# Sum of ReLU rows: the last 128 rows one to a partition, their sums turned by a transposition and stored in four packets

## The chip, the cores and the metric

One core of a Trainium2 chip. The metric is the device time of one execution in microseconds (us); the kernel before takes 160.97 us, the median of three runs (160.88 to 161.13). ACT is the scalar engine, DVE the vector engine, POOL is GpSimd, SP is the engine that issues all transfers here.

## The reference

```python
# x: float32, 32 x 512 x 1024
relu_x = np.maximum(x, 0)
return np.sum(relu_x, axis=-1).astype(np.float32)     # 32 x 512
```

So 16,384 rows of 1,024 numbers are clamped at zero and each is summed: 67.11 MB are read and 64 KB are written.

## The kernel before

The input is seen as 16,384 rows. The first 2,048 rows are cut so that each of the 128 partitions has 16 rows that lie one behind another in memory (`xf`, line 83). The other 14,336 are cut in the same way into 112 rows for each partition (`xv`, line 84). The sums of a partition stand in a row of the SBUF tensor `res` (128 x 128), in the same order, and so each store writes one piece of memory for each partition.

The loop over `TWO` (lines 183 to 203) works through seven blocks of 16 rows for each partition, 8 MB each, in three buffers in turn. ACT clamps a piece in place (`clamp`, line 144), and DVE sums its rows (`total`, line 152). Of the last two blocks, some rows are done in a single pass: ACT clamps and sums a row in one instruction (`act_row`, line 159), and so does DVE (`dve_row`, line 167). Both write the sum with a second short instruction that reads the engine's accumulator. Then come two smaller loads of 8 and 4 rows (`TAIL`, lines 208 to 218), whose rows alternate between ACT and DVE.

The last four rows of each partition are four loads (lines 220 to 245), all issued on SP's one queue, in this order. Sizes are bytes for each partition:

- 9,208: two whole rows and the first 254 numbers of the third. ACT and DVE do one row each, POOL clamps the 254 numbers (line 234).
- 3,492: the last 873 numbers of the fourth row. ACT sums 321 and DVE 552 of them (`act_part` line 121, `dve_part` line 126).
- 2,072: the next 518 numbers of the third row, 214 on ACT, 304 on DVE.
- 1,612: the last 403 numbers, which end the third row (252 of them) and begin the fourth (151), into a tensor `last` that has free columns at both ends. The partial sums above were written into those columns.

When this last load and all five partial results are there (one semaphore, `all_there`, line 253), DVE's line 254 adds the clamped `last` half to the 254 numbers from POOL and gives the sum of row three, while ACT's line 121 gives the sum of row four. There is no instruction after that: both sums land in two neighbouring columns of `res`.

There are three stores (`store`, line 115), all issued by SP behind all the loads: the first 16 columns (64 bytes for each partition), the next 110 columns (440 bytes), and the last two columns (8 bytes, 128 packets, line 264). SP holds the last of these until DVE and ACT have written. After it SP clears the semaphores, waits until the three stores have landed (line 51), and the kernel is over. `wait_ge` is a wait that is an instruction by itself; `wait_op` hangs a wait on an instruction. The first load is issued ahead of the kernel's opening (line 268).

Of the kernel before, what the change touches and what calls it, by code (L numbers as in the profile page):

```python
# [4 lines left out]
F32 = mybir.dt.float32  # L5
RELU = mybir.ActivationFunctionType.Relu
MAX, ADD = mybir.AluOpType.max, mybir.AluOpType.add
P = 128

ROWS = 16  # L10
# [10 lines left out]

HEAD, MIDDLE = 254, 518
LAST_DVE, LAST_ACT = 252, 151
MIDDLE_ACT, END_ACT = 214, 321

EARLY = 1

# [1 line left out]
def kernel(tc: tile.TileContext, x: bass.AP, out: bass.AP):  # L31
    nc = tc.nc
    sems = Semaphores(tc)

    tc.close()
    tc.compile()
    nc.cur_bb = nc.bb_map[tc.start_bb_name]
    body = nc.cur_bb.bb.instructions
    ends = list(body)
    body.clear()  # L40
    n_stores = relu_sum(nc, sems, x, out)
    body.extend(ends)


    nc.cur_bb = nc.bb_map[tc.start_bb_name + "_end"]
    nc.cur_bb.bb.instructions.clear()
    nums = sorted(s.num for s in (*sems.loads, sems.act, sems.dve))
    cleared = range(nums[0], nums[-1] + 1)
    assert len(cleared) == len(nums)
    nc.sync.sem_clear(cleared)  # L50
    nc.sync.wait_ge(sems.stored, 16 * n_stores).then_inc(sems.stored, -16 * n_stores)
    open_without_barrier(tc, EARLY)


class Semaphores:
    def __init__(self, tc: tile.TileContext):
        n = len(TWO) + len(TAIL) + 4
        self.loads = [tc.alloc_semaphore(f"load{i}") for i in range(n)]
        self.act = tc.alloc_semaphore("act")
        self.dve = tc.alloc_semaphore("dve")  # L60
        self.end = self.loads[-1]
        self.stored = tc.alloc_semaphore("stored")


def relu_sum(nc, sems: Semaphores, x: bass.AP, out: bass.AP):
    x_flat = x.flatten_outer_dims()
    N, D = x_flat.shape
    NT = N // P
    NB = len(TWO)
    assert N == P * NT == P * ROWS * (NB + 1)  # L70
    assert sum(TAIL) == ROWS - 4
    assert HEAD + MIDDLE + LAST_DVE == D and HEAD == 2 + LAST_DVE

    bufs = [nc.alloc_sbuf_tensor(f"io{i}", [P, ROWS, D], F32) for i in range(NBUF)]
    res = nc.alloc_sbuf_tensor("res", [P, NT], F32)


    n_last = LAST_DVE + LAST_ACT
    last = nc.alloc_sbuf_tensor("last", [P, 2 + n_last + 2], F32)


    N1 = P * ROWS
    xf = x_flat[:N1].rearrange("(p m) d -> p m d", p=P)
    xv = x_flat[N1:].rearrange("(p m) d -> p m d", p=P)
    o_flat = out.rearrange("b s -> (b s)")
    of = o_flat[:N1].rearrange("(p m) -> p m", p=P)
    ov = o_flat[N1:].rearrange("(p m) -> p m", p=P)

    def rows(m, n):
        if m < ROWS:  # L90
            return xf[:, m : m + n, :]
        return xv[:, m - ROWS : m - ROWS + n, :]

    def sums(m, n):
        if m < ROWS:
            return of[:, m : m + n], res[:, m : m + n]
        return ov[:, m - ROWS : m - ROWS + n], res[:, m : m + n]
# [3 lines left out]
    def load(dst, src, after=None):  # L101
        nonlocal n_load
        dma = nc.sync.dma_start(out=dst, in_=src)  # L103
        if after:
            dma.wait_op(sems.dve, after[1], "sem-ge")
        dma.then_inc(sems.loads[n_load], 16)
        n_load += 1
        return sems.loads[n_load - 1]

    def store(m, n, act, sem, count):  # L110
        nonlocal n_store
        dst, src = sums(m, n)
        if act:
            nc.sync.wait_ge(sems.act, act)
        nc.sync.dma_start(out=dst, in_=src).wait_op(sem, count, "sem-ge").then_inc(
            sems.stored, 16
        )
        n_store += 1

    def act_part(ap, accum_out, after):  # L120
        nc.scalar.activation(out=ap, in_=ap, func=RELU, accum_out=accum_out).wait_op(  # L121
            *after, "sem-ge"
        ).then_inc(sems.end, 1)

    def dve_part(ap, accum_out, after):
        i = nc.vector.tensor_scalar(  # L126
            out=ap,
            in0=ap,
            scalar1=0.0,
            scalar2=None,  # L130
            op0=MAX,
            op1=ADD,
            accum_out=accum_out,
        )
        if after is not None:
            i.wait_op(*after, "sem-ge")
        i.then_inc(sems.end, 1)

    def clamp(ap, loaded):
        nonlocal n_act  # L140
# [16 lines left out]
    def act_row(ap, accum_out, loaded):  # L157
        nonlocal n_act
        i = nc.scalar.activation(out=ap, in_=ap, func=RELU, accum_out=accum_out)  # L159
        if loaded is not None:  # L160
            i.wait_op(loaded, 16, "sem-ge")
        i.then_inc(sems.act, 1)
        n_act += 1

    def dve_row(ap, accum_out, loaded):
        nonlocal n_dve
        i = nc.vector.tensor_scalar(  # L167
            out=ap,
            in0=ap,
            scalar1=0.0,  # L170
            scalar2=None,
            op0=MAX,
            op1=ADD,
            accum_out=accum_out,
        )
        if loaded is not None:
            i.wait_op(loaded, 16, "sem-ge")
        i.then_inc(sems.dve, 1)
        n_dve += 1

    freed = []
    m = 0
    for j in range(NB):
        buf = bufs[j % NBUF]
        loaded = load(buf[:, :, :], rows(m, ROWS), j >= NBUF and freed[j - NBUF])
        c = 0
# [20 lines left out]
    c = 0  # L207
    for n in TAIL:
        loaded = load(
            buf[:, c : c + n, :], rows(m, n), None if c else freed[NB - NBUF]  # L210
        )
# [6 lines left out]
            m += 1  # L218

    flat = buf[:, :, :].rearrange("p c d -> p (c d)")  # L220
    src = rows(m, 4).rearrange("p c d -> p (c d)")
    at = c * D
    head = 2 * D + HEAD
    middle = head + MIDDLE
    end = middle + n_last


    loaded = load(flat[:, at : at + head], src[:, :head])
    act_row(buf[:, c, :], res[:, m : m + 1], loaded)
    sums_act = n_act  # L230
    dve_row(buf[:, c + 1, :], res[:, m + 1 : m + 2], loaded)
    sums_dve = n_dve
    clamped = flat[:, at + 2 * D : at + head]
    nc.gpsimd.tensor_scalar(  # L234
        out=clamped, in0=clamped, scalar1=0.0, scalar2=None, op0=MAX
    ).wait_op(loaded, 16, "sem-ge").then_inc(sems.end, 1)
    for lo, hi, n, first, second in (
        (end, 4 * D, END_ACT, 2 + n_last, 3 + n_last),
        (head, middle, MIDDLE_ACT, 0, 1),
    ):  # L240
        loaded = load(flat[:, at + lo : at + hi], src[:, lo:hi])
        act_part(flat[:, at + lo : at + lo + n], last[:, first : first + 1], (loaded, 16))
        dve_part(flat[:, at + lo + n : at + hi], last[:, second : second + 1], (loaded, 16))
    loaded = load(last[:, 2 : 2 + n_last], src[:, middle:end])
    assert loaded is sems.end

    store(0, ROWS, freed[0][0], sems.dve, freed[0][1])
    store(ROWS, NT - ROWS - 2, sums_act, sems.dve, sums_dve)  # L250


    all_there = (sems.end, 16 + 5)
    nc.vector.scalar_tensor_tensor(  # L254
        out=clamped,
        in0=last[:, : 2 + LAST_DVE],
        scalar=0.0,
        in1=clamped,
        op0=MAX,
        op1=ADD,  # L260
        accum_out=res[:, NT - 2 : NT - 1],
    ).wait_op(*all_there, "sem-ge").then_inc(sems.end, 1)
    act_part(last[:, 2 + LAST_DVE :], res[:, NT - 1 : NT], all_there)
    store(NT - 2, 2, 0, sems.end, 16 + 5 + 2)
    return n_store


def open_without_barrier(tc: tile.TileContext, n_loads: int):

    SP = mybir.EngineType.SP
    blocks = tc.nc.main_func.blocks
    opening = blocks[0].instructions
    body = next(b for b in blocks if b.name == tc.start_bb_name).instructions
    for i in list(opening):
        if isinstance(i, (mybir.InstDrain, mybir.InstEventSemaphore)):
            opening.remove(i)
    loads = [i for i in body if i.engine == SP][:n_loads]
    for i in loads:  # L280
        assert isinstance(i, mybir.InstDMACopy)
        body.remove(i)
    at = next(n for n, i in enumerate(opening) if i.engine == SP)
    opening[at:at] = loads
# [30 lines left out]
```

## Time and profile before

| what | value |
|---|---|
| median of three runs | 160.97 us (160.88 to 161.13) |
| span of the profiled execution, first to last instruction | 159.695 us (the page rounds to 159.7) |
| what lies around the span, median less span | 1.27 us |
| DMA engines busy | 98.0% of the span, 421 GB/s |
| DVE, ACT, POOL busy | 118.8, 103.6, 1.0 us |
| last load landed, by the trace's semaphore records | 157.749 us |
| last store issued on SP, and landed | 158.262 us, 159.661 us |

Only the span is given of the profiled execution; its own time outside the profiler isn't, so the 1.27 us is a difference between the median and the span. A row of a timeline is the start, the length, the engine, the line and the shape of an instruction, all in us from the span's start. SPq is SP's issue of a transfer; the transfer itself goes on after it. The trace also holds each packet that a DMA engine moved, with its start and size, and the moment at which each engine's semaphore increment arrived.

### The profile page before, as it was taken

The page shows a single profiled execution, that of the slowest core. Times are in us where ns is not written, and L with a number is a line of the kernel's source. Part 1 is how long each engine was busy: PE and PEld are TensorE (multiplying, and loading weights), DVE is VectorE, ACT ScalarE, POOL GpSimd, SP SyncE. Part 2 cuts the span into 40 slices and gives each one's busy share as a digit, 9 for nine tenths or more (in the row PEclk, how much of TensorE's full clock was granted, in tenths as well). Part 3 has the DMA queues.
Part 4 walks back from the last instruction along what each step waited for, and adds up shares of the span by engine and source line. Part 5 has one row for each costly group of instructions (what it writes and reads, how often), then busy time and mean ns, then how long its engine had stood idle before and what let it go on. Part 6 is the DMA issues. An engine that isn't in the chain of part 4 may idle for free.

```text
span 159.7 us, 125 instructions
## 1 busy us (share of the span) xinstructions
DVE 118.8 (74%) x44; ACT 103.6 (65%) x53; POOL 1.0 (1%) x5
## 2 busy tenths in 40 slices
DVE  0000000006999799999999999999999799999986
ACT  0000049993699808996099951999329993496995
POOL 0000000000000000000000000000000000000001
DMA  7996996996997997979969969969969969898993
GB/s 263 525 525 263 525 509 279 525 509 279 525 476 312 525 443 345 525 328 460 525 279 509 525 263 525 525 263 525 509 279 525 492 295 525 353 435 386 407 409 128
DMA packets 2304, 67.18 MB, mean 421 GB/s; under 512 B 640, under 2 KB 768, under 8 KB 1024
## 3 DMA queue, kind: packets, MB, share of 16 engines
q1 hardware_dynamic: 2304, 67.18, 98.0%
HBM read 67.11 MB, written 0.07 MB: 421 GB/s over the span
## 4 chain that ended last, share of the span: by engine, by line
DVE 45%; DMA 45%; ACT 9%; SPq 1%; issue 0%
DMA io<-in_x_dram 45%; DVE res L152 43%; ACT io L144 9%; DVE io L167 1%; SPq L103 1%; DVE io L126 1%; DVE io L254 0%
## 5 line engine op out<-in xcount | busy, mean ns | idle before, releaser
L152 DVE TENSOR_REDUCE res<-io 128x8 f32<-128x8192 f32 (+2 forms) x10 | 101.1, 10175 | 38.9 <-ACT io L144 38.9
L144 ACT ACTIVATE io<-io 128x8192 f32<-128x8192 f32 (+2 forms) x10 | 81.8, 8218 | 25.9 <-DMA io<-in_x_dram 25.9
L159 ACT ACTIVATE io<-io 128x1024 f32<-128x1024 f32 x18 | 18.8, 1043 | 6.6 <-DMA io<-in_x_dram 6.6
L167 DVE TENSOR_SCALAR_CACHE_REDUCE io<-io 128x1024 f32<-128x1024 f32 x14 | 16.2, 1214 | 0.5 <-DMA io<-in_x_dram 0.4
L142 ACT ACT_TABLE_LOAD x1 | 1.3, 1283 | 22.0 <-DMA io<-in_x_dram 22.0
L159 ACT ACTIVATION_READ_ACCUMULATOR io<-io 128x1 f32 x18 | 3.4, 187 | 0.0
L234 POOL TENSOR_SCALAR io<-io 128x254 f32<-128x254 f32 x1 | 0.8, 840 | 155.1 <-DMA io<-in_x_dram 155.1
L167 DVE DVE_READ_ACCUMULATOR io<-io 128x1 f32 x14 | 1.1, 82 | 0.0
L126 DVE TENSOR_SCALAR_CACHE_REDUCE io<-io 128x552 f32<-128x552 f32 (+1 forms) x2 | 1.1, 596 | 0.0
L121 ACT ACTIVATE io<-io 128x321 f32<-128x321 f32 (+1 forms) x2 | 0.9, 426 | 0.1
L254 DVE SCALAR_TENSOR_TENSOR io<-last,io 128x254 f32<-128x254 f32 x1 | 0.4, 425 | 0.0
L121 ACT ACTIVATION_READ_ACCUMULATOR io<-io 128x1 f32 x2 | 0.4, 187 | 0.0
L121 ACT ACTIVATE last<-last 128x153 f32<-128x153 f32 x1 | 0.3, 332 | 0.0
L121 ACT ACTIVATION_READ_ACCUMULATOR last<-last 128x1 f32 x1 | 0.2, 187 | 0.0
L126 DVE DVE_READ_ACCUMULATOR io<-io 128x1 f32 x2 | 0.2, 84 | 0.0
L299 POOL MEMSET const-bfloat16-1.0<- 128x1 bf16 x1 | 0.1, 101 | 0.0
L299 POOL MEMSET const-uint8-127<- 128x1 uint8 x1 | 0.1, 101 | 0.0
L299 POOL MEMSET const-float32-0.0<- 128x1 f32 x1 | 0.1, 99 | 0.2 <-issue 0.2
L299 POOL MEMSET const-float32-1.0<- 128x1 f32 x1 | 0.1, 98 | 0.0
L254 DVE DVE_READ_ACCUMULATOR io<-last,io 128x1 f32 x1 | 0.1, 83 | 0.0
## 6 DMA issues: line engine op xcount, KB each, us to landing
io<-in_x_dram SPq DMA_DIRECT2D x1, 4096.0 KB, 23.8
io<-in_x_dram SPq DMA_DIRECT2D x1, 2048.0 KB, 28.3
io<-in_x_dram SPq DMA_DIRECT2D x1, 1151.0 KB, 30.6
io<-in_x_dram SPq DMA_DIRECT2D x1, 436.5 KB, 31.2
io<-in_x_dram SPq DMA_DIRECT2D x1, 259.0 KB, 31.4
last<-in_x_dram SPq DMA_DIRECT2D x1, 201.5 KB, 31.4
io<-in_x_dram SPq DMA_DIRECT2D x7, 29.1
out_dram<-res SPq DMA_DIRECT2D x1, 55.0 KB, 1.6
```

What stands on the lines that cost most here:

```text
L103: dma = nc.sync.dma_start(out=dst, in_=src)
L121: nc.scalar.activation(out=ap, in_=ap, func=RELU, accum_out=accum_out).wait_op(*after, "sem-ge").then_inc(sems.end, 1)
L126: i = nc.vector.tensor_scalar(out=ap, in0=ap, scalar1=0.0, scalar2=None, op0=MAX, op1=ADD, accum_out=accum_out,)
L142: nc.scalar.preload_act_table(RELU).wait_op(loaded, 16, "sem-ge")
L144: i = nc.scalar.activation(out=ap, in_=ap, func=RELU)
L152: nc.vector.tensor_reduce(out=res[:, m : m + n], in_=ap, axis=mybir.AxisListType.X, op=ADD).wait_op(sems.act, n_act, "sem-ge").then_inc(se ...
L159: i = nc.scalar.activation(out=ap, in_=ap, func=RELU, accum_out=accum_out)
L167: i = nc.vector.tensor_scalar(out=ap, in0=ap, scalar1=0.0, scalar2=None, op0=MAX, op1=ADD, accum_out=accum_out,)
L234: nc.gpsimd.tensor_scalar(out=clamped, in0=clamped, scalar1=0.0, scalar2=None, op0=MAX).wait_op(loaded, 16, "sem-ge").then_inc(sems.end, 1)
L254: nc.vector.scalar_tensor_tensor(out=clamped, in0=last[:, : 2 + LAST_DVE], scalar=0.0, in1=clamped, op0=MAX, op1=ADD, accum_out=res[:, NT ...
L299: nc = _bacc.Bacc("TRN2", target_bir_lowering=False, num_devices=1)
```

## The change

The partition cut of the 14,336 rows becomes one of 14,208: each partition has 111 rows of them, and the last 128 rows of the input (`xl`) are given one to each partition. Of the last four rows of a partition, the third is now finished before the last, from the 254 numbers that POOL clamped (DVE, `scalar_tensor_tensor`), its 516 last numbers (ACT) and an addition of both on POOL. The fourth, from `xl`, comes in two loads of 573 and 451 numbers. The loads of the end are therefore 9,208, 3,080, 2,292 and 1,804 bytes for each partition, again four.

The sum of that last row is made of two halves, as before a piece on ACT (180 numbers) and a piece on DVE (271 numbers and the two partial sums of the first 573). Then DVE adds the halves into column 0 of `column`, a 128 x 32 tensor that POOL zeroed at the start, and transposes it in blocks of 32 x 32 into `across`. Row 0, 32, 64 and 96 of `across` hold 32 sums each, which are neighbours in the output. The last store writes these four rows, 128 bytes each, instead of 8 bytes from each of 128 partitions. The second store now carries 111 columns (444 bytes) and waits for POOL's addition.

```diff
@@ -21,9 +21,11 @@
-HEAD, MIDDLE = 254, 518
-LAST_DVE, LAST_ACT = 252, 151
-MIDDLE_ACT, END_ACT = 214, 321
+HEAD = 254
+HEAD_ACT = 516
+FIRST, FIRST_ACT = 573, 240
+LAST_ACT = 180
+BLOCK = 32
 EARLY = 1
@@ -44,7 +46,7 @@
     nc.cur_bb = nc.bb_map[tc.start_bb_name + "_end"]
     nc.cur_bb.bb.instructions.clear()
-    nums = sorted(s.num for s in (*sems.loads, sems.act, sems.dve))
+    nums = sorted(s.num for s in (*sems.loads, sems.act, sems.dve, sems.pool, sems.fin))
     cleared = range(nums[0], nums[-1] + 1)
     assert len(cleared) == len(nums)
     nc.sync.sem_clear(cleared)
@@ -58,6 +60,8 @@
         self.loads = [tc.alloc_semaphore(f"load{i}") for i in range(n)]
         self.act = tc.alloc_semaphore("act")
         self.dve = tc.alloc_semaphore("dve")
+        self.pool = tc.alloc_semaphore("pool")
+        self.fin = tc.alloc_semaphore("fin")
         self.end = self.loads[-1]
         self.stored = tc.alloc_semaphore("stored")
@@ -69,22 +73,29 @@
     NB = len(TWO)
     assert N == P * NT == P * ROWS * (NB + 1)
     assert sum(TAIL) == ROWS - 4
-    assert HEAD + MIDDLE + LAST_DVE == D and HEAD == 2 + LAST_DVE
+    assert HEAD + HEAD + HEAD_ACT == D
     bufs = [nc.alloc_sbuf_tensor(f"io{i}", [P, ROWS, D], F32) for i in range(NBUF)]
     res = nc.alloc_sbuf_tensor("res", [P, NT], F32)
-    n_last = LAST_DVE + LAST_ACT
-    last = nc.alloc_sbuf_tensor("last", [P, 2 + n_last + 2], F32)
+    n_last = D - FIRST
+    split = nc.alloc_sbuf_tensor("split", [P, FIRST], F32)
+    last = nc.alloc_sbuf_tensor("last", [P, 2 + n_last], F32)
+    halves = nc.alloc_sbuf_tensor("halves", [P, 4], F32)
+    column = nc.alloc_sbuf_tensor("column", [P, BLOCK], F32)
+    across = nc.alloc_sbuf_tensor("across", [P, BLOCK], F32)
     N1 = P * ROWS
     xf = x_flat[:N1].rearrange("(p m) d -> p m d", p=P)
-    xv = x_flat[N1:].rearrange("(p m) d -> p m d", p=P)
+    N2 = N - P
+    xv = x_flat[N1:N2].rearrange("(p m) d -> p m d", p=P)
+    xl = x_flat[N2:]
     o_flat = out.rearrange("b s -> (b s)")
     of = o_flat[:N1].rearrange("(p m) -> p m", p=P)
-    ov = o_flat[N1:].rearrange("(p m) -> p m", p=P)
+    ov = o_flat[N1:N2].rearrange("(p m) -> p m", p=P)
+    ol = o_flat[N2:].rearrange("(b i) -> b i", i=BLOCK)
     def rows(m, n):
         if m < ROWS:
@@ -116,25 +127,6 @@
             sems.stored, 16
         )
         n_store += 1
-
-    def act_part(ap, accum_out, after):
-        nc.scalar.activation(out=ap, in_=ap, func=RELU, accum_out=accum_out).wait_op(
-            *after, "sem-ge"
-        ).then_inc(sems.end, 1)
-
-    def dve_part(ap, accum_out, after):
-        i = nc.vector.tensor_scalar(
-            out=ap,
-            in0=ap,
-            scalar1=0.0,
-            scalar2=None,
-            op0=MAX,
-            op1=ADD,
-            accum_out=accum_out,
-        )
-        if after is not None:
-            i.wait_op(*after, "sem-ge")
-        i.then_inc(sems.end, 1)
     def clamp(ap, loaded):
         nonlocal n_act
@@ -178,6 +170,7 @@
         i.then_inc(sems.dve, 1)
         n_dve += 1
+    nc.gpsimd.memset(column[:, :], 0.0).then_inc(sems.pool, 1)
     freed = []
     m = 0
     for j in range(NB):
@@ -218,50 +211,77 @@
             m += 1
     flat = buf[:, :, :].rearrange("p c d -> p (c d)")
-    src = rows(m, 4).rearrange("p c d -> p (c d)")
+    src = rows(m, 3).rearrange("p c d -> p (c d)")
     at = c * D
     head = 2 * D + HEAD
-    middle = head + MIDDLE
-    end = middle + n_last
+    end = 3 * D
     loaded = load(flat[:, at : at + head], src[:, :head])
     act_row(buf[:, c, :], res[:, m : m + 1], loaded)
-    sums_act = n_act
     dve_row(buf[:, c + 1, :], res[:, m + 1 : m + 2], loaded)
-    sums_dve = n_dve
     clamped = flat[:, at + 2 * D : at + head]
     nc.gpsimd.tensor_scalar(
         out=clamped, in0=clamped, scalar1=0.0, scalar2=None, op0=MAX
-    ).wait_op(loaded, 16, "sem-ge").then_inc(sems.end, 1)
-    for lo, hi, n, first, second in (
-        (end, 4 * D, END_ACT, 2 + n_last, 3 + n_last),
-        (head, middle, MIDDLE_ACT, 0, 1),
-    ):
-        loaded = load(flat[:, at + lo : at + hi], src[:, lo:hi])
-        act_part(flat[:, at + lo : at + lo + n], last[:, first : first + 1], (loaded, 16))
-        dve_part(flat[:, at + lo + n : at + hi], last[:, second : second + 1], (loaded, 16))
-    loaded = load(last[:, 2 : 2 + n_last], src[:, middle:end])
-    assert loaded is sems.end
-
-
-
-    store(0, ROWS, freed[0][0], sems.dve, freed[0][1])
-    store(ROWS, NT - ROWS - 2, sums_act, sems.dve, sums_dve)
-
-
-    all_there = (sems.end, 16 + 5)
+    ).wait_op(loaded, 16, "sem-ge").then_inc(sems.pool, 1)
+
+
+    loaded = load(flat[:, at + head : at + end], src[:, head:end])
+    act_row(flat[:, at + head + HEAD : at + end], halves[:, 1:2], loaded)
+    raw = flat[:, at + head : at + head + HEAD]
+    nc.vector.wait_ge(sems.pool, 2)
     nc.vector.scalar_tensor_tensor(
         out=clamped,
-        in0=last[:, : 2 + LAST_DVE],
+        in0=raw,
         scalar=0.0,
         in1=clamped,
         op0=MAX,
         op1=ADD,
-        accum_out=res[:, NT - 2 : NT - 1],
-    ).wait_op(*all_there, "sem-ge").then_inc(sems.end, 1)
-    act_part(last[:, 2 + LAST_DVE :], res[:, NT - 1 : NT], all_there)
-    store(NT - 2, 2, 0, sems.end, 16 + 5 + 2)
+        accum_out=halves[:, 0:1],
+    ).wait_op(loaded, 16, "sem-ge").then_inc(sems.dve, 1)
+    n_dve += 1
+    nc.gpsimd.wait_ge(sems.act, n_act)
+    nc.gpsimd.tensor_tensor(
+        out=res[:, m + 2 : m + 3], in0=halves[:, 0:1], in1=halves[:, 1:2], op=ADD
+    ).wait_op(sems.dve, n_dve, "sem-ge").then_inc(sems.pool, 1)
+
+
+    loaded = load(split[:, :], xl[:, :FIRST])
+    act_row(split[:, :FIRST_ACT], last[:, 0:1], loaded)
+    dve_row(split[:, FIRST_ACT:], last[:, 1:2], loaded)
+    loaded = load(last[:, 2:], xl[:, FIRST:])
+    assert loaded is sems.end
+
+
+    store(0, ROWS, freed[0][0], sems.dve, freed[0][1])
+    store(ROWS, NT - ROWS - 1, 0, sems.pool, 3)
+
+
+    cut = 2 + n_last - LAST_ACT
+    nc.scalar.activation(
+        out=last[:, cut:], in_=last[:, cut:], func=RELU, accum_out=halves[:, 2:3]
+    ).wait_op(loaded, 16, "sem-ge").then_inc(sems.fin, 1)
+    nc.vector.wait_ge(sems.act, n_act)
+    nc.vector.wait_ge(sems.dve, n_dve)
+    nc.vector.tensor_scalar(
+        out=last[:, :cut],
+        in0=last[:, :cut],
+        scalar1=0.0,
+        scalar2=None,
+        op0=MAX,
+        op1=ADD,
+        accum_out=halves[:, 3:4],
+    ).wait_op(loaded, 16, "sem-ge").then_inc(sems.fin, 1)
+    nc.vector.tensor_tensor(
+        out=column[:, 0:1], in0=halves[:, 2:3], in1=halves[:, 3:4], op=ADD
+    ).wait_op(sems.fin, 2, "sem-ge").then_inc(sems.fin, 1)
+    nc.vector.transpose(out=across[:, :], in_=column[:, :]).wait_op(
+        sems.fin, 3, "sem-ge"
+    ).then_inc(sems.fin, 1)
+    nc.sync.dma_start(out=ol, in_=across[::BLOCK, :]).wait_op(
+        sems.fin, 4, "sem-ge"
+    ).then_inc(sems.stored, 16)
+    n_store += 1
     return n_store
```

## The prediction

> **What bounds the kernel now.** I read the page's first three parts, then the chain that ended last, then the timeline of the last 4 us, then SP's waits. The first three say that the transfers are the bound:
>
> ```profile
> span 159.7 us, 125 instructions
> DVE 118.8 (74%) x44; ACT 103.6 (65%) x53; POOL 1.0 (1%) x5
> q1 hardware_dynamic: 2304, 67.18, 98.0%
> ```
>
> The one queue that everything goes through keeps its engines busy for 98.0% of the span, while DVE has 26% of it free. The trace's packet records show the pace: a 65,536-byte packet takes 2.418 us, 27.1 bytes per ns on each of 16 engines. So no change to compute matters until the last load has landed; the change doesn't take a byte away. What can move the end is what stands behind that landing. The timeline shows it:
>
> ```profile
> 156.73 1.86 SPq L115 DMA_DIRECT2D out_dram<-res  x2
> ...
> 157.29 0.38 ACT L121 ACTIVATE io<-io 128x214 f32<-128x214 f32 x1
> 157.29 0.47 DVE L126 TENSOR_SCALAR_CACHE_REDUCE io<-io 128x304 f32<-128x304 f32 x1
> 157.58 0.19 ACT L121 ACTIVATION_READ_ACCUMULATOR io<-io 128x1 f32 x1
> 157.69 0.08 DVE L126 DVE_READ_ACCUMULATOR io<-io 128x1 f32 x1
> 157.80 0.33 ACT L121 ACTIVATE last<-last 128x153 f32<-128x153 f32 x1
> 157.80 0.42 DVE L254 SCALAR_TENSOR_TENSOR io<-last,io 128x254 f32<-128x254 f32 x1
> 158.04 0.19 ACT L121 ACTIVATION_READ_ACCUMULATOR last<-last 128x1 f32 x1
> 158.15 0.08 DVE L254 DVE_READ_ACCUMULATOR io<-last,io 128x1 f32 x1
> ```
>
> The last load's final semaphore increment arrives at 157.749 by the trace. Both engines start 0.05 us later, at 157.80, and end at 158.23 and 158.235. SP's issue of the last store starts at 158.262 (the second half of the first row above), 0.027 us behind DVE. What follows is the store alone:
>
> ```profile
> SPq L115 <- DVE io L254: 1.2, 1, 1.2
> ...
> L115 SPq DMA_DIRECT2D out_dram<-res x3: 332/344/404, 126.9 to 158.3; - x3
> ...
> out_dram<-res SPq DMA_DIRECT2D x1, 1.0 KB, 1.4
> ```
>
> SP waited 1.2 us for DVE, issued in 0.332 us, and the 1.0 KB landed 1.4 us after the issue began: 158.262 to 159.661. SP's end follows 0.034 us later, at 159.695. So behind the landing lie 0.054 + 0.432 of compute, 0.027 of handing over, 1.399 of store and 0.034 of end: 1.946 us. My sum is on these.
>
> The packet records split the store's 1.399: 0.825 from the start of the issue to the first packet (159.087), 0.189 to the start of the last of 128 packets (159.276; each engine has eight, of 9 ns), some 0.006 to the last semaphore packet (159.282), then 0.379 to the last increment.
>
> **The loads.** The four last loads carried 9,208 + 3,492 + 2,072 + 1,612 bytes for each partition and will carry 9,208 + 3,080 + 2,292 + 1,804, the same 16,384 in the same four packets. Packets of the old sizes took 347, 139, 86 and 68 ns, which is 8.5 ns + bytes/27.1; the three new ones come to 122, 93 and 75, 290 against 293. Eight to an engine, that is 0.02 us less: I put the last landing at 157.75 as before. The two between come at about 156.45 and 157.19 (156.586 - 8 x 0.017, and 157.266 - 8 x 0.010). The partitions' distance in memory falls from 112 rows to 111, and the last 128 rows lie one row apart. The first block, 16 rows apart, runs at the same 2.418 us a packet as the rest, at 112 rows, so I cost the new distances at nothing; the price of an error there stands under the rivals.
>
> **What is to be ready before the last landing.** ACT starts the row of 1,024 at 155.48 as before, and can begin the 516 numbers at 156.54. By its slope of 0.83 ns (381 ns for 214, 471 for 321) its result is written at 157.27; then 240 numbers from 157.25 to 157.745. DVE does the 254 pairs from 156.65 to 157.15, and 333 numbers from 157.24 to 157.76 (304 took 0.395 to the accumulator read, plus 29 x 1.042 ns, plus 0.083). POOL's addition starts near 157.32. It is bounded by 0.10 us (a POOL memset of 128x1) and 0.84 (its clamp of 254); even with 0.84 SP can issue the 444-byte store at 158.2 and be free at 158.55, and I need SP at 158.7. So this store stays under cover, with 0.15 us to spare; if it isn't, what it takes longer goes straight onto the end. POOL's memset at the start lies in 155 us of idle POOL.
>
> **The chain behind the landing, step by step.**
> 1. DVE now has two waits of their own ahead of its last piece, one for ACT's sums (157.745) and one for its own accumulator (157.76). Nothing else is queued behind them but the end's chain. No DVE wait of that kind is in the trace. Below: nothing, if both pass before 157.80. Above: SP's rows, where a 17 ns wait was followed by the next instruction 52 ns later, 0.07 for each, so a start at 157.92. I take 0.05 late, 157.85, as the sums come so near to the landing.
> 2. The pieces: 273 on DVE take 0.363 + 0.083 = 0.446; 180 on ACT 0.26 + 0.187, from 157.80 to 158.25. DVE ends at 158.30, against 158.235.
> 3. **Addition** of 128x1. Not in the trace. Nearest below: the 0.082 of an accumulator read. Above: DVE's whole-instruction rows less their elements, 425 - 254 x 1.042 = 160 ns, 470 - 304 x 1.042 = 153. As what follows waits for the written result, I take 0.155, and 0.025 for the semaphore (the 0.027 of DVE to SP): 158.48.
> 4. **Transposition** of 128x32. Also not there; below 0.082 + 0.033, above 0.425 (the 254-wide row). I take 0.155 + 32 x 1.042 ns = 0.19, and 0.025: 158.695. The Trainium skill ("VectorE: DVE Perf Modes", The three transpose paths) gives 311 ns for 128x128 of a 2-byte type; an estimate from it, 96 columns fewer, is 0.21, and the sum would be 0.02 longer.
> 5. **The store**: issue at 158.72 with SP's 0.027. Four packets in place of 128: I take 0.19 off the 1.399, the time between the first and the last of an engine's packets, as no engine has more than one. Landed at 158.72 + 1.21 = 159.93; end 159.965.
>
> Span +0.27 us. With the 1.27 us around it (160.97 less 159.695; the page gives no more on the profiled execution itself) and the median it is 160.97 + 0.27 = **161.24 us**, 0.17% slower, which is about the size of the spread of the three runs, and within the 0.2% that a measurement can tell.
>
> Bounds of the unknown terms: waits -0.05 to +0.07 around my value, addition -0.07 to +0.03, transposition -0.08 to +0.23, and the store's part below.
>
> **The rivals.**
> - *The store gets no shorter* (the other side: slower by more than can be missed). If the 1.399 us are latency of a store whatever it carries, the two new DVE steps and the waits are paid in full: 0.065 + 0.18 + 0.215 = 0.46, so 161.43, +0.29%. For it: 64-, 440- and 8-byte packets all show 0.33 to 0.38 us from semaphore packet to increment, and the 440-byte store also needs 0.837 to its first packet. Against: the 0.189 of packets is plainly there. It decides from the point where the store saves under 0.14 us. Chance 0.20. The Trainium skill speaks for it ("DMA: Bandwidth & Descriptors", Anatomy of one DMA): the fixed cost of a transfer is mostly the wait for the write's receipt, and not its setup. This trace has 0.38 of receipt against 0.83 before the first packet, so it bears the rule out only in part.
> - *The time before the first packet shrinks too.* Of the 0.825, 0.332 is SP's own and 0.49 lies between SP's end and the packet. If a part of the 0.49 is the writing of 128 packets' descriptors, up to some 0.3 more goes: 160.9 to 161.05. No store with fewer packets is in the trace. Chance 0.18.
> - *Both at their ends*: the steps at their floors (0.014 + 0.10 + 0.14 = 0.25) and all of 0.49 + 0.19 saved: -0.43, 160.55, faster. Chance 0.06.
> - *The last rows' reads are slower.* 128 rows one row apart lie in 512 KB, and the 16 engines may get in each other's way. The last two loads are 8 x 168 ns on an engine; a quarter more is 0.34 us, 161.6. Against: equal packet times at both distances. Chance 0.06.
> - *The store still lands as 16 pieces.* The Trainium skill (same page, Why a DMA increments its semaphore by 16 and not by 1) says that a transfer whose slowest dimension is four uses four engines, the issuing engine giving the other twelve increments at once. The trace of before has only 128-partition transfers, each with 16 increments. If it is cut into 16 it would cost at most the 16 increments' 10 ns steps, 0.12 us, inside my forecast's own range.
>
> **Chances.** Forecast 0.50, own range 161.05 to 161.42, of which a third lies over 161.29. Slower by over 0.2%: 0.16 + 0.18 + 0.06 = 0.40. Faster (under 160.65): 0.06. Within: 0.54. The range of 160.85 to 161.55 takes in the forecast, the first rival, most of the second and leaves out the floor of all and the dear reads.
>
> **What would show it.** In the changed profile: last landing at 157.75; DVE's last piece at 157.80 to 157.92; an addition of about 0.155 and a transposition near 0.19; four 128-byte packets some 0.82 us behind the issue, and the store's landing in 1.2 rather than 1.4. I would be wrong if the store lands under 1.05 us, if DVE's two steps take under 0.25 together, or if the last landing moves by more than 0.1.

## The result, and the profile after

The changed kernel takes 161.71 us (161.66 to 161.76, four runs), the kernel before 161.03 us beside it: 1.0039 times as long, 95% interval 1.0027 to 1.0051. It is slower by 0.68 us, and the forecast of 161.24 with its range up to 161.55 was too low. The profiled span grew by as much, from 159.695 to 160.372 us.

The page of the changed kernel answers to the three lines of before. The transfers are the bound as they were, and DVE has two more instructions:

```profile
span 160.4 us, 131 instructions
DVE 118.9 (74%) x46; ACT 103.7 (65%) x53; POOL 1.3 (1%) x7
q1 hardware_dynamic: 2168, 67.18, 97.6%
```

The last load's final increment arrives at 157.667 us (157.749 before). So the time is lost behind that moment. The timeline of the changed kernel's last stretch (start, length, engine, line) shows all of it:

```profile
157.54 0.34 SPq L126 DMA_DIRECT2D out_dram<-res  x1
157.57 0.08 DVE L159 DVE_READ_ACCUMULATOR split<-split 128x1 f32 x1
157.69 0.35 ACT L261 ACTIVATE last<-last 128x180 f32<-128x180 f32 x1
157.80 0.44 DVE L266 TENSOR_SCALAR_CACHE_REDUCE last<-last 128x273 f32<-128x273 f32 x1 [0.15 <-DMA last<-in_x_dram]
157.95 0.19 ACT L261 ACTIVATION_READ_ACCUMULATOR last<-last 128x1 f32 x1
158.16 0.08 DVE L266 DVE_READ_ACCUMULATOR last<-last 128x1 f32 x1
158.28 0.16 DVE L275 TENSOR_TENSOR column<-halves 128x1 f32<-128x1 f32 x1
158.48 0.21 DVE L278 STREAM_TRANSPOSE across<-column 128x32 f32<-128x32 f32 x1
158.72 0.63 SPq L281 DMA_DIRECT2D out_dram<-across  x1
```

ACT starts 0.02 us behind the landing, DVE 0.11 later than ACT. It isn't the landing that DVE starts from. The chain that ended last shows what it starts from (start, length, what; the load of 573 numbers writes `split`, and L265 is the wait by itself, a single instruction for both of the waits in the diff):

```profile
125.77 31.35 DMA split<-in_x_dram
157.12 0.02 issue
157.14 0.52 DVE split L159 x2
157.66 0.03 issue
157.69 0.05 DVEq L265
157.74 0.07 issue
157.80 0.46 DVE last L266 x2
```

DVE's work on the load before ends at 157.649, 0.018 us ahead of the last landing, and the wait with the gaps around it takes 0.154 us from there to 157.803. In all six runs with these instructions the wait starts 0.039 to 0.040 us behind the end of that work, wherever the landing falls (0.004 to 0.023 ahead of the wait); the timeline's row of L266 names the load as releaser only because its increment came last. So the last load, which landed 0.08 us earlier than in the kernel before, was not what DVE waited for; a shorter piece of DVE on the 573 numbers might give back up to 0.11 us (an estimate, DVE's start less ACT's), which no run tried. Then come the addition, the transposition, and in the last row something that the forecast doesn't have: SP needs 0.63 us to issue the four packets, where the 128 packets of before took 0.332. In the packet records the first packet follows 1.230 us behind the start of that issue (0.825 before), and the last increment 1.619 us behind it (1.399 before). The store with 4 packets takes 0.22 us longer than the one with 128.

From the landing to the end, by the trace's records in us:

| | before | forecast | after |
|---|---|---|---|
| last load landed | 157.749 | 157.75 | 157.667 |
| landing to the start of DVE's last piece | 0.054 | 0.10 | 0.136 |
| that piece | 0.432 | 0.446 | 0.446 |
| addition with its semaphore | – | 0.18 | 0.194 |
| transposition with its semaphore | – | 0.215 | 0.249 |
| DVE to SP | 0.027 | 0.027 | 0.028 |
| start of the issue to the last increment | 1.399 | 1.21 | 1.619 |
| increment to the end | 0.034 | 0.034 | 0.033 |

DVE's part, with the handing over to SP, grew by 0.540 (some 0.46 forecast), the store by 0.220 (-0.19 forecast), and the landing came 0.082 earlier: together 0.677, the whole growth of the span.

### The profile page after: what moved, and what is told of

The parts are those of the page before. It is cut to its first block, busy times and chain, and to the rows that moved or that the text cites. A ratio compares the mean times of both kernels' runs of the same rounds, so it can differ in the third digit from the quotient of the medians.

```text
span 160.4 us, 131 instructions
## 1 busy us (share of the span) xinstructions
DVE 118.9 (74%) x46; ACT 103.7 (65%) x53; POOL 1.3 (1%) x7
## 4 chain that ended last, share of the span: by engine, by line
DMA 45%; DVE 44%; ACT 9%; SPq 1%; issue 0%; DVEq 0%
DVE res L144 43%; DMA io<-in_x_dram 25%; DMA split<-in_x_dram 20%; ACT io L136 9%; SPq L114 1%; DVE split L159 0%; DVE last L266 0%; DVE across L278 0%; DVE column L275 0%; DVEq L265 0%
## 5 line engine op out<-in xcount | busy, mean ns | idle before, releaser
L151 ACT ACTIVATE io<-io 128x1024 f32<-128x1024 f32 (+1 forms) x19 | 19.4, 1022 | 6.6 <-DMA io<-in_x_dram 6.6
L159 DVE TENSOR_SCALAR_CACHE_REDUCE split<-split 128x333 f32<-128x333 f32 x1 | 0.5, 502 | 0.2 <-DMA split<-in_x_dram 0.2
L266 DVE TENSOR_SCALAR_CACHE_REDUCE last<-last 128x273 f32<-128x273 f32 x1 | 0.4, 441 | 0.2 <-DMA last<-in_x_dram 0.2
```

The source lines that it names most:

```text
L159: i = nc.vector.tensor_scalar(out=ap, in0=ap, scalar1=0.0, scalar2=None, op0=MAX, op1=ADD, accum_out=accum_out,)
L266: nc.vector.tensor_scalar(out=last[:, :cut], in0=last[:, :cut], scalar1=0.0, scalar2=None, op0=MAX, op1=ADD, accum_out=halves[:, 3:4],).wa ...
```

## The experiments: why is the store of four packets longer?

Each run changes only the last store, of the kernel before or of the changed one, unless it is said otherwise. "Store" is the time from the start of SP's issue to the last increment; each such figure comes from one profiled execution. Several of these kernels store only a part of the sums, or wrong ones; they are for measuring the store alone. The code cuts show two runs side by side where they can, with `...` for what is left out. The letters K, S, F and T stand for theories that the expectation of the first run names, N and M for later ones.

**First four runs: count, step or first use.** The edits, one in each kernel:

```diff
 # run b4: before, every 32nd partition       run b16: the same with ::8
-    store(NT - 2, 2, 0, sems.end, 16 + 5 + 2)
+    nc.sync.dma_start(out=dst[::32, :], in_=src[::32, :])...
 # run a16: changed kernel, 16 packets of 32 bytes
-    nc.sync.dma_start(out=ol, in_=across[::BLOCK, :])...
+    nc.sync.dma_start(out=o_flat[N2:].rearrange("(b i) -> b i", i=8), in_=across[::8, :8])...
 # run warm4: changed kernel, one transfer more, ahead of the stores
+    nc.sync.dma_start(out=spare[::BLOCK, :], in_=column[::BLOCK, BLOCK:])...
```

> The kernel before, with its last store cut to every 32nd partition: 4 packets of 8 bytes; the sums of the other 124 partitions' last two rows are not stored. Theory K (a transfer with fewer than 16 packets costs SP longer: it has to account for the engines that take no part): the issue takes 0.63 us instead of 0.33, the store 1.6 instead of 1.40, span about 159.9. Theory S (a source that steps over partitions costs SP longer): the same here. Theory F (the first transfer of a new form costs once): the same here. Theory T (what is new lies in the transposed tensor or in the DVE steps ahead of the store): issue 0.33, store 1.2, span 159.5.

> The kernel before, with its last store cut to every 8th partition: 16 packets of 8 bytes, one to an engine; the other 112 partitions' last two sums are not stored. K: issue 0.33 us, the store 0.19 us shorter than the 1.40 before (1.21), span 159.5. S: issue 0.63, store about 1.5 to 1.6, span 159.8 to 159.9. F: 0.63 too, if a step over partitions makes a new form; 0.33 if only the number of engines does.

> The changed kernel, with its last store taken from every 8th partition, 8 numbers each: 16 packets of 32 bytes; the sums stored are not those of the rows in order. Everything ahead of the store is as in the changed kernel. K: issue 0.33, store 1.2, span 160.37 - 0.40 = 159.97, which is the forecast's sum; time about 161.3. S: 0.63 and span 160.3.

> The changed kernel, with one more transfer of the same form (4 partitions, step 32, 128 bytes, from zeroed columns to a spare tensor) issued by SP some 30 us ahead of the stores. F: that one takes 0.63 us to issue and the last store 0.33, store 1.2 to 1.3, span near 160.0. K and S: both take 0.63, span 160.37 as the changed kernel.

SP's issue in the four kernels, from their timelines: the kernel before with 4 and with 16 packets, the changed one with 16 packets, and the one with a transfer ahead (its first row is that transfer, the second its last store):

```profile
158.17 0.63 SPq L265 DMA_DIRECT2D out_dram<-res  x1
```

```profile
158.24 0.56 SPq L265 DMA_DIRECT2D out_dram<-res  x1
```

```profile
158.59 0.56 SPq L281 DMA_DIRECT2D out_dram<-across  x1
```

```profile
126.74 0.63 SPq L257 DMA_DIRECT2D spare<-column  x1
...
158.74 0.56 SPq L286 DMA_DIRECT2D out_dram<-across  x1
```

All four are long, and the first packet comes 1.19 to 1.22 us behind the issue in each. The first line alone rules out theory T: with nothing transposed and no instruction added on DVE, the kernel before gets the long issue too. K, my favourite, falls with the second and third: 16 packets take all 16 engines (16 increments, one from each) and the issue is still 0.56. F explains at most 0.07: the second transfer of the same form took 0.556 where the first took 0.630. The times of whole kernels, each against the kernel before run beside it (ratio, 95% interval), are less sharp: b4 161.16 against 160.98 (1.0008, 0.9998 to 1.0018, so not told from no change), b16 161.26 (1.0017, 1.0007 to 1.0026), a16 161.86 (1.0052, 1.0037 to 1.0067), warm4 161.64 (1.0040, 1.0025 to 1.0055). The last two are no faster than the changed kernel (1.0039). Theory S, the step over partitions, was left.

**Next four runs: step or count.** The sources are now neighbours, or not, with the same number of packets:

```diff
 # run a4near: changed kernel                  run adirect: the changed kernel, no transposition
-    ... in_=across[::BLOCK, :]                 -    nc.vector.transpose(out=across[:, :], ...)
+    ... in_=across[0:4, :]                     +    ... in_=column[:, 0:1]
 # run n64: before, partitions 0 to 63          run s64: before, every 2nd partition
+    ... in_=src[0:64, :]                       +    ... in_=src[::2, :]
```

> The changed kernel, with its last store taken from partitions 0 to 3 of the transposed tensor in place of 0, 32, 64 and 96: again 4 packets of 128 bytes; three of the four rows stored are not sums. Theory S (a source that steps over partitions makes the issue long): issue 0.33 us, first packet 0.83 us behind the issue, span 160.37 - 0.40 = 159.97. Theory N (any transfer that isn't of 128 partitions): issue 0.56 to 0.63, first packet 1.2 behind, span 160.3 to 160.4.

> The kernel before, with its last store cut to partitions 0 to 63: 64 packets of 8 bytes; the other 64 partitions' last two sums are not stored. S: issue 0.33, first packet 0.83 behind it, span 159.6 to 159.7. N: issue 0.56 to 0.63, first packet 1.2 behind, span 160.0 to 160.1.

> The kernel before, with its last store cut to every 2nd partition: 64 packets of 8 bytes; the other 64 partitions' last two sums are not stored. S and N: issue 0.56 to 0.63, first packet 1.2 behind it, span 160.0 to 160.1. If the step must be at least 8, or a small count is what matters: 0.33 and 159.6.

> The changed kernel without the transposition: the last store takes the 128 sums straight from the column that DVE's addition writes, 128 packets of 4 bytes. S and N alike: issue 0.33, first packet 0.83 behind it, store 1.40 as before; span 160.37 - 0.24 (transposition) - 0.22 (store) = 159.9, time about 161.2: slower than before by the addition and the waits alone.

The last store's issue, of a4near, n64 and s64 in this order:

```profile
158.97 0.33 SPq L281 DMA_DIRECT2D out_dram<-across  x1
```

```profile
158.31 0.54 SPq L265 DMA_DIRECT2D out_dram<-res  x1
```

```profile
158.33 0.54 SPq L265 DMA_DIRECT2D out_dram<-res  x1
```

With four neighbouring partitions the issue is back at 0.332 us, the first packet 0.756 behind it, and the store is 1.144, shorter than before's 1.399 and near the forecast's 1.21. That is as S says. But n64 contradicts S: 64 neighbouring partitions have no step, and the issue is 0.536 with the first packet at 1.174, just like every second partition. N fails on a4near. (a4near 161.29, 1.0021, 1.0011 to 1.0030; n64 161.35, 1.0022, 1.0013 to 1.0031; s64 161.27, 1.0021, 1.0012 to 1.0031. All were compared with 160.97.) So neither theory held all four, and I looked at what the compiled programs say of these transfers. Each transfer may carry a mark there, `ant_dge_precooked`:

```
last store of       source                              mark
before              res    [[128,128],[1,2]]            true
changed kernel      across [[1024,4],[1,32]]            none
a4near              across [[32,4],[1,32]]              true
n64                 res    [[128,64],[1,2]]             none
```

A source is given here as pairs of step and count in numbers; a partition of `res` holds 128 numbers and one of `across` 32, so that `[1024,4]` is every 32nd partition and `[32,4]` four neighbours. Every transfer of the kernel before has the mark, all loads and all three stores. The changed kernel's last store is the only transfer in it that has none; the same goes for b4, b16, a16, n64 and s64, and in warm4 it is both four-packet transfers. All long issues so far are unmarked and all short ones marked. I call a marked issue "prepared" after the name of the mark; what it makes SP leave out no run shows, only what it is worth. In programs that were compiled only, the last store of the kernel before got no mark with any of five steps over partitions (2 to 32), and with neighbouring partitions it got it for fifteen of sixteen counts from 1 to 128, all but 64; what is special about 64 I don't know.

**Last four runs: the mark by itself.** Two runs take the mark off a store that has it, by a switch of the language around that one line; nothing else differs in the compiled program from before and from a4near:

```diff
 # run boff: before                             run near4off: the same around a4near's store
+    nc.dge_precook = False
     store(NT - 2, 2, 0, sems.end, 16 + 5 + 2)
+    nc.dge_precook = True
 # run n16: before, partitions 0 to 15          run b1col: before, one column of two
+    ... in_=src[0:16, :]                       +    dst, src = sums(NT - 1, 1)
```

> The kernel before with one bit changed: the compiler's mark for a prepared issue is taken off the last store; the transfer itself is the same, 128 packets of 8 bytes. Theory M (what makes an issue long is that the transfer doesn't carry that mark): issue 0.54 to 0.56 us, first packet 1.2 behind it, span 159.695 + 0.38 = 160.08, time +0.35 us. If step or count are what matters: no change, 159.7.

> The changed kernel with its store taken from four neighbouring partitions, as in the run where the issue took 0.33 us, but with the mark taken off this store; three of the four rows stored are not sums. M: issue 0.56 to 0.63, first packet 1.2 behind it, and the store lands 0.45 later than the 1.144 there, about 1.6, as in the changed kernel. If the step of 32 partitions were the cause by itself: 0.33 and 1.15.

> The kernel before with its last store cut to partitions 0 to 15: 16 packets of 8 bytes, which carry the mark; the other 112 partitions' last two sums are not stored. M: issue 0.33, first packet 0.76 to 0.83 behind it. If fewer packets shorten a store as forecast: landed 1.2 us behind the issue in place of 1.40, span 159.5. If the 16 engines' start spreads the packets all the same: 1.3 and 159.6.

> The kernel before with only its very last column stored: 128 packets of 4 bytes, 448 bytes apart in the output; the 128 sums of the column beside it are not stored. In the changed kernel without the transposition, 128 packets of 4 bytes that are neighbours in the output took 7.1 us to land. If the 4-byte size is what costs: 6 to 7 us again, span 165. If it is that neighbouring packets share a stretch of memory: 1.40 us and span 159.7.

The issue in boff, near4off, n16 and b1col:

```profile
158.19 0.54 SPq L115 DMA_DIRECT2D out_dram<-res  x1
```

```profile
158.85 0.74 SPq L282 DMA_DIRECT2D out_dram<-across  x1
```

```profile
158.15 0.34 SPq L265 DMA_DIRECT2D out_dram<-res  x1
```

```profile
158.02 0.33 SPq L265 DMA_DIRECT2D out_dram<-res  x1
```

That settles it for the mark. The same store of 128 packets of 8 bytes takes 1.399 us with the mark and 1.756 without; the issue grows from 0.332 to 0.542 and the first packet moves from 0.825 to 1.179. The time of the kernel before goes from 161.00 to 161.32 by that bit alone (1.0018, 1.0010 to 1.0027). The store of four neighbouring partitions goes from 1.144 to 1.722, and the kernel takes 161.87 us (1.0052, 1.0037 to 1.0067), no faster than the changed one. Its issue of 0.736 is longer than the 0.56 to 0.63 that M gave. The transposed tensor isn't the cause, since a4near's store from it is short. Nor does the step cost anything of its own that these runs show: of the two unmarked stores of 64 packets the one with a step takes 0.02 us longer, and near4off, without a step, takes longer than the changed kernel with it. The step decides whether the transfer gets the prepared issue. Cutting the store to 16 packets or to one column, with the mark, can't be told in the time: n16 160.85 (0.9992, 0.9984 to 1.0001), b1col 160.91 (0.9999, 0.9989 to 1.0008).

The stores of all kernels, in us from the start of the issue:

| store | mark | issue | first packet | last packet | landed |
|---|---|---|---|---|---|
| before, 128 packets | yes | 0.332 | 0.825 | 1.020 | 1.399 |
| n16, 16 | yes | 0.340 | 0.833 | 0.987 | 1.328 |
| a4near, 4 | yes | 0.332 | 0.756 | 0.822 | 1.144 |
| b1col, 128 of 4 bytes | yes | 0.333 | 0.826 | 1.021 | 1.410 |
| adirect, 128 of 4 bytes | yes | 0.332 | 0.827 | 1.017 | 7.149 |
| boff, 128 | no | 0.542 | 1.179 | 1.374 | 1.756 |
| n64, 64 | no | 0.536 | 1.174 | 1.341 | 1.696 |
| s64, 64 | no | 0.542 | 1.179 | 1.349 | 1.713 |
| b16, 16 | no | 0.563 | 1.210 | 1.357 | 1.700 |
| a16, 16 | no | 0.557 | 1.202 | 1.350 | 1.701 |
| b4, 4 | no | 0.629 | 1.224 | 1.291 | 1.603 |
| after, 4 | no | 0.631 | 1.230 | 1.295 | 1.619 |
| warm4, 4, second of its form | no | 0.556 | 1.186 | 1.252 | 1.581 |
| near4off, 4 | no | 0.736 | 1.328 | 1.394 | 1.722 |

The last packet of a row can be the one that carries an increment. The 7.149 of adirect is told of in the last section. One thing stays open: unmarked issues on four engines spread from 0.556 to 0.736 us, those on sixteen only from 0.536 to 0.563, so a store of four partitions may cost up to 0.2 us of its own without the mark. First use may account for 0.07 of that, by warm4; the 0.736 of near4off isn't explained.

## Why the prediction was wrong

**Step 5, the store, is the step that failed, and it failed in its sign.** It took 0.19 us off 1.399, because no engine has more than one packet; measured are +0.220. Two things were wrong in it. The larger is what it held fixed: "issue at 158.72 with SP's 0.027" took over SP's 0.332 and the 0.493 up to the first packet from the rows of before's own transfers, three stores and thirteen loads, all of which are issued in the prepared way. The new store isn't, and this costs 0.405 to the first packet (1.230 - 0.825). That the source steps over partitions stood in the diff, `across[::BLOCK, :]`, and no row of before had such a source. I bounded the time before the first packet only from below ("up to some 0.3 more goes") and not from above.

The smaller is the 0.19 itself. With the mark, 16 packets on 16 engines land after 1.328, 0.07 less than 128 packets: one packet to an engine still spreads over 0.154 us (0.833 to 0.987), since the engines don't start together. Only using four engines brings it to 1.144, 0.255 less. So a shortening of the size that I forecast exists, but it comes with few engines; few packets on each gave only 0.07.

**Steps 1 to 4 had the right costs with small errors of size, and step 1 hung DVE's start on the wrong event.** The waits made DVE 0.11 us later than ACT (157.803 against 157.690), where I had taken 0.05. Forecast were 0.09 us from DVE's sum (157.76) to its next start (157.85), with 0.16 as the upper bound; measured are 0.154 (157.649 to 157.803). The one wait instruction took 0.050 and the next started 0.065 behind it, 0.115 together against the 0.07 that SP's rows had shown. And it was this chain on DVE that set the start, not the last landing, which I had as the moment that all else counts from. The addition took 0.159 (0.155 forecast), the transposition 0.214 (0.19; the estimate from the Trainium skill's 311 ns for a larger one, "VectorE: DVE Perf Modes", The three transpose paths, was 0.21 and the closer). Each handing over by a semaphore on DVE took 0.035, not 0.025. Counted from the landing, all this together is 0.08 more than forecast.

**The loads** were costed rightly at nothing: the landing moved by 0.08, and the runs with the kernel before's loads put it between 157.53 and 157.82, those with the changed ones between 157.56 and 157.93. The rival with dear reads came nearest in time (161.6), but its reason, a landing 0.34 us later, is out. **POOL's addition** took 0.193 us, and its store was issued at 157.54, well under cover.

**The rivals.** Of the others "the store gets no shorter" came nearest, at 161.43, but not for its reason: the store isn't a fixed latency. The Trainium skill's account of it ("DMA: Bandwidth & Descriptors", Anatomy of one DMA), in a section on transfers that GpSimd issues, is that most of the fixed cost is the wait for the write's receipt. The traces here, of transfers that SP issues, don't agree: 0.31 to 0.39 us of 1.14 to 1.76 lie between the last packet and the last increment, whatever the store carries but for the run told of below; what moved was ahead of the first packet. "The time before the first packet shrinks too" is right by 0.07 for a marked transfer on four engines (0.756) and wrong by 0.4 for the one that was made. The store did use four engines, with one early increment for the other twelve, as the same page of the Trainium skill says (Why a DMA increments its semaphore by 16 and not by 1); the records show one arrival at 159.728 and four from 160.279 on.

With a marked store the forecast's time would have held, in part by luck: a4near, whose steps ahead of the store are those of the changed kernel, came 0.32 us behind before (161.29 against 160.97), where 0.27 was forecast. Behind its landing it is the 0.27, since two errors of 0.065 cancel: the steps up to SP's issue cost 0.526 more (some 0.46 forecast) and the store 0.255 less (0.19 forecast). It isn't a way out, because it stores other rows. Even a marked store of 1.144 saves 0.255, and the steps that it needs cost 0.526 there and 0.540 in the changed kernel. So no version of this change that the runs show beats the kernel before.

## What to carry to other kernels

A store at the very end is paid from the start of its issue, so look at how the issue is made before counting packets: here the compiler's mark, which no store from partitions that aren't neighbours got, was worth 0.36 to 0.58 us (boff, near4off), more than 128 packets cost against four (0.255). When a diff brings a transfer of a form that no row of the trace has, the time of its issue is an unknown with bounds on both sides, and the compiled program can tell whether it is issued like the others. Two short instructions behind the last load cost 0.44 us with their semaphores, for 0.034 us of work on their 33 elements (an estimate at 1.04 ns for each, the slope between DVE's rows of 17,222 ns for 16,384 elements and 8,679 ns for 8,192); what they make possible must save more.

## What the runs showed of the hardware that was not expected

- The run without the transposition stored 128 sums as 128 packets of 4 bytes, neighbours in the output, with a marked issue of 0.332 and the last packet started at 1.017 us; yet the increments came from 3.377 to 7.149 us, and the kernel took 167.08 us (1.0383 times before, 1.0367 to 1.0398), where 161.2 was expected. Packets of the same 4 bytes 448 bytes apart (b1col) landed after 1.410 us. The size is not the cause; that the packets lie next to each other in memory is the likely cause, and it isn't shown by itself: the two stores also differ in the tensor they come from and in the kernel around them. In adirect the second store, of 444 bytes, is still under way when the last is issued (it lands 0.65 us later); but so it is in a4near, whose last store lands after 1.144. Which part of the memory path makes the packets wait was not tried. So the transposition is worth some 5.3 us (spans of 165.638 and 160.372) once the last rows lie one to a partition; the cut of before doesn't need it.

The line that shows it is adirect's row of transfers from issue to landing, against b1col's:

```profile
DMA to landing us min/median/max: 7.1/7.1/7.1
```

```profile
DMA to landing us min/median/max: 1.4/1.4/1.4
```

- The start of a store's packets is no plain function of their number. With marked issues, 128 packets were all started within 0.195 us, 16 within 0.154, four within 0.066.
